# Attention's last steps, early compression weights, 32-row prompt norms and an earlier output projection in a hybrid decoder layer

## The chip, the cores and the metric

The kernel runs on one core of a Trainium2 chip, as one launch. The metric is the device time of the launch in microseconds; the table below has three runs and one profiled execution.

## The reference, cut to what matters

One inference step of one decoder layer, for a prompt of 512 tokens and for 8 samples of 4 tokens with 2048 past tokens. Every output is wanted in fp32.

```python
h = rmsnorm(x, w['g_mix'])
q, kc_new, ..., xm, vm, om, i_pre, f_pre = split_cols(h @ w['w_in'])
k_cmp = compress(kc_all, *w['cmp_k'])     # per 16-token block: two halves @ w1, gelu, @ w2
v_cmp = compress(vc_all, *w['cmp_v'])
o_nsa = nsa_attend(q, k_cmp, v_cmp, ks_all, vs_all, kw_all, vw_all, gates, offset, w_pre)
o_nsa = rmsnorm(o_nsa, w['g_head_nsa'])   # norm over the 64 columns of each of 8 heads
hm, C, n, m = mlstm_chunked(qm, km, vm, i_pre + w['b_i'], f_pre + w['b_f'], C0, n0, m0)
x = x + concatenate([o_nsa, gated_headnorm(hm)]) @ w['w_out']
x = x + cross_attention(rmsnorm(x, w['g_xa'])) @ w['w_xo']
x = x + swiglu(rmsnorm(x, w['g_ffn']))
```

`nsa_attend` adds three softmax attentions with gates: over compressed blocks, over selected 64-token blocks, over a window of 512. `mlstm_chunked` is a gated linear recurrence with 4 heads of 128.

## The kernel before, in words

**Numbers.** Products that must be exact to fp32 are made of three reduced-precision matmuls. `split(hi, lo, src)` (L212) writes a rounded copy `hi` on ACT (L213) and the rest `lo` on DVE or POOL (L214); `mm3` (L216) issues hi·hi, lo·hi and hi·lo (L218 to L220). A weight tile of 128x1024 is thus split by one ACT and one DVE instruction before TensorE (PE) may use it.

**Order of the work.** A scheduler writes one list of instructions per engine, and every engine then runs its list strictly in order. Program order counts, `tc.high_priority(offset)` pulls a block ahead of it, and `tc.issue_after(ins)` holds a block behind an instruction. The stages are generators: `weave(bg, fg)` (L315) runs a background generator of dense matmuls and takes a step of a foreground generator whenever the credit allows it, so that vector work of one stage lies beside matmuls of another.

**Stages, by time in the profile.** Projections and prompt attention (0 to 240 us), the hand-over to the prompt's mLSTM and to `compress(0)` (230 to 258), the compression of the samples' keys and then values (`compress(0)`, `compress(1)`, 254 to 535) woven with the mLSTM of prompt and samples and with the samples' attention, the end of the samples' attention (535 to 591), the projection by `w_out`, cross-attention (about 700 to 835) and SwiGLU.

**Prompt attention, `nsa` (L603).** 32 units (j, i, br), that is four head pairs j, four query tiles i and two branches; each has two heads v. `score` makes scores on PE, their minimum on DVE (L621), the exponential on ACT (L623), and the scaling by gate and sum on POOL (L625, tile `sb`). `turned` transposes `sb` on PE (L634) and copies it to `PT` on ACT (L636). `value` multiplies `PT` with the values (L646). In each step of the loop the transposes of v = 1 come first, then the `value` of an earlier pair of units, then the transposes of v = 0. After a pair's fourth tile its result goes to `oF` (L208 by DVE in the profile).

**mLSTM, `mlstm` (L766).** `load_qk(h)` (L778) loads two 128x128 weights `wqk` of a head in one buffer; `proj` projects with them (L799, L802) and asks for the next head's when the second of the two is used. `gate` (L811, L817, L818) makes the decay matrix, L825 and L827 the scores.

**Compression, `compress(kv)` (L1121).** 8 blocks b (the samples) of 4 steps t. `weights(t)` (L1125) splits the 128x1024 weight of a step into `w1h` and `w1l` and adds its halves on POOL (`ws`, L1134). `produce(b, t)` (L1171) transposes the gathered block on DVE (`xf`, L1191), splits it into `xh` and `xl`, and adds halves on POOL (`xs`, L1198); the steps are produced two ahead of the matmuls (L218 to L220 and L1296). `prompt_cols` (L1166) reads the prompt's rows back from a scratch array in memory (`xf<-cd`, issued by SP) and transposes them (`ys`, L1168). In the last block of `compress(0)` SP also loads the values' weights (`wr`, L588).

**The samples' selected blocks, `sample` (L1418).** For each key/value head g: keys are transposed by PE (L1518) and copied to `kt` by ACT or DVE (`keys`, L206 or L208), multiplied with the queries (L1528), and 2048 columns go through four exponentials on ACT (L1701). Then, for each g, the probabilities are transposed (L1518) and copied to `PTs`, and multiplied with the gathered values (L1722).

**The prompt's norms, `finals_p` (L1391).** For each head pair j: the compressed branch by two matmuls of 64 rows (L1398), added to `oF` (L1401), squared on ACT (L1402) into 512 columns of a tile of 128x2048; a matmul with `bones` (L1407, ones on the two 64x64 diagonal blocks, scaled) makes the mean square, copied back by ACT (L1408). Then one logarithm (L1411) and one exponential (L1412) over 2048 columns, each with a load of its table, and four products on DVE (L1415). It runs between the values of g = 0 and of g = 1.

**Output projection.** `early_mix` (L1824) splits `oF` into the projection's moving operand (`mh`, `ml`), and the first half of the columns (hf = 0) is multiplied with the splits of `w_out` (`whi`, `wlo`); `close_sample` and `load_xT` (L1811) transpose the residual `x`.

## Time and profile before

| | us |
|---|---|
| three runs | 1231.31, 1234.45, 1232.87 (median 1232.87) |
| the profiled execution, its own time | 1243.24 |
| its span on the core | 1241.5 |
| PE busy (share of the span) | 1174.3 (95%) |
| VectorE (DVE), ScalarE (ACT), GpSimd (POOL) busy | 841.2, 612.4, 558.6 |
| mean granted clock of PE | 0.974 |

The profiled execution is 10.4 us above the median of the runs, and 1.7 us of its time lie outside the span. PE is busy nearly throughout, so one reads the places where it isn't: a window that shows its busy time below the window's length, or a granted clock (column PEclk) below 1.00. PEld is the load of the stationary operand and runs beside PE. "Waits" names what released an engine that had stood. In windows and groups "x8" counts instructions; a matmul of fp32 operands stands there as two.

### The profile page before, as it was taken

Reading aid. Unit: us, or ns where it says so; the run is one execution under the profiler, and the core shown is the slowest. Engines: PE = TensorE matmul, PEld = TensorE weight load, DVE = VectorE, ACT = ScalarE, POOL = GpSimd, SP = SyncE. Lnnn points to the kernel's source line nnn. Section 1 sums busy time; section 2 is a strip of 40 time slices with the busy share of each in tenths; the row PEclk is TensorE's granted clock in tenths of the full one; section 3 lists DMA queues with packets and bytes.
Section 4 is the critical chain, followed back from the end, with each engine's and each line's share of the span. In section 5 each row is a group of like instructions: output and inputs, shape, how many; then the busy total and the mean of one; then the engine's idle time right before and its main releaser. Section 6 shows DMA issues by size and latency. Waiting matters only on the chain.

```text
span 1241.5 us, 24581 instructions
## 1 busy us (share of the span) xinstructions
PE 1174.3 (95%) x9220; PEld 1066.7 (86%) x9220; DVE 841.2 (68%) x1901; ACT 612.4 (49%) x1414; POOL 558.6 (45%) x686
## 2 busy tenths in 40 slices
PE   7999999899997989988999989999899999999996
PEld 5998999588885878854999987599899999999996
DVE  6337683567787687653754756554998888888874
ACT  5235665745545444466542423342665565555452
POOL 1013353566666266542342100043885576476342
PEclk9999999899997999999999998999999999999998
DMA  7324240141253185566767298630032333322411
GB/s 232 102 53 105 86 153 1 51 137 44 78 171 115 42 283 176 178 227 205 206 135 171 83 239 288 231 128 2 1 119 86 103 96 107 106 94 77 137 52 73
DMA packets 141769, 154.30 MB, mean 124 GB/s; under 512 B 17449, under 2 KB 123689, under 8 KB 141394
## 3 DMA queue, kind: packets, MB, share of 16 engines
q1 hardware_dynamic: 131922, 119.17, 32.0%
q0 software_dynamic: 9728, 33.56, 8.3%
q8 instruction: 73, 1.20, 0.4%
q14 instruction: 46, 0.38, 0.1%
HBM read 141.67 MB, written 13.12 MB: 125 GB/s over the span
## 4 chain that ended last, share of the span: by engine, by line
PE 49%; DVE 8%; ACT 3%; DMA 2%; issue 2%; SPq 1%; POOL 1%; POOLq 0%; DVEq 0%; ACTq 0%
PE xc L2291 7%; PE xa L2291 7%; PE bd L2291 5%; PE tp L2291 5%; PE bd L220 3%; PE bd L219 3%; PE bd L218 3%; DVE sp L2231 1%; DMA mkv<-in_cache_mem_k 1%; PE xa L1296 1%; PE tp L1518 1%; PE bd L2190 1%; PE xa L218 1%; PE xa L219 1%; PE xa L220 1%
## 5 line engine op out<-in xcount | busy, mean ns | idle before, releaser
L214 POOL TENSOR_TENSOR al<-fraw,ah 128x512 fp32r<-128x512 f32 (+1 forms) x104 | 127.5, 1227 | 152.4 <-ACT ah L213 124.0
L213 ACT ACTIVATE whi<-wraw 128x1024 fp32r<-128x1024 f32 (+3 forms) x74 | 62.5, 890 | 57.5 <-DMA wraw<-in_w_xv 28.2
L214 DVE TENSOR_TENSOR wlo<-wraw,whi 128x1024 fp32r<-128x1024 f32 (+3 forms) x74 | 73.6, 1026 | 19.1 <-ACT whi L213 19.0
L213 ACT ACTIVATE ah<-fraw 128x512 fp32r<-128x512 f32 (+1 forms) x112 | 65.8, 593 | 38.0 <-PE xc L2291 11.8
L218 PE MATMUL bd<-w1h,xh 128*128 128x256 f32 x256 | 82.6, 325 | 0.9 <-issue 0.9
L220 PE MATMUL bd<-w1h,xl 128*128 128x256 f32 x256 | 75.6, 298 | 3.0 <-DVE xl L214 3.0
L1198 POOL TENSOR_TENSOR xs<-xf 128x256 f32<-128x256 f32 x64 | 55.8, 878 | 50.2 <-PE xa L1296 30.5
L219 PE MATMUL bd<-w1l,xh 128*128 128x256 f32 x256 | 75.7, 297 | 0.0
L1296 PE MATMUL xa<-ws,xs 128*128 128x256 f32 x256 | 71.2, 400 | 2.4 <-DVE bq L1470 1.3
L625 POOL TENSOR_SCALAR sb<-sb,rs,gat 128x128 f32<-128x128 f32 (+3 forms) x64 | 46.1, 724 | 54.4 <-DVE rs L624 40.2
L213 ACT ACTIVATE xh<-xf 128x512 fp32r<-128x512 f32 x64 | 40.0, 629 | 45.5 <-DVE xf L1191 20.0
L213 ACT ACTIVATE ah<-sp 128x512 fp32r<-128x512 f32 (+1 forms) x64 | 35.5, 555 | 50.1 <-DVE sp L2231 22.8
L220 PEld LDWEIGHTS bd<-w1h,xl 128*128 128x128 f32 x256 | 48.9, 192 | 6.4 <-DVE xl L214 3.8
L1296 PEld LDWEIGHTS xa<-ws,xs 128*128 128x128 f32 x256 | 46.5, 201 | 8.5 <-issue 2.9
L218 PEld LDWEIGHTS bd<-w1h,xh 128*128 128x128 f32 x256 | 49.1, 193 | 5.0 <-issue 3.9
L214 DVE TENSOR_TENSOR xl<-xf,xh 128x512 fp32r<-128x512 f32 x64 | 47.5, 746 | 8.6 <-ACT xh L213 7.7
L219 PEld LDWEIGHTS bd<-w1l,xh 128*128 128x128 f32 x256 | 49.4, 193 | 4.5 <-issue 2.8
L219 PE MATMUL bd<-hlo,whi 128*128 128x272 f32 x176 | 52.0, 296 | 0.0
L218 PE MATMUL bd<-hhi,whi 128*128 128x272 f32 x176 | 51.7, 294 | 0.0
L1191 DVE STREAM_TRANSPOSE xf<-cgat 128x512 f32<-128x512 f32 x64 | 44.7, 703 | 10.2 <-POOL xs L1198 8.4
L220 PE MATMUL bd<-hhi,wlo 128*128 128x272 f32 x176 | 51.3, 292 | 0.0
L2231 DVE TENSOR_TENSOR sp<-fraw 128x512 f32<-128x512 f32 (+1 forms) x32 | 47.8, 1494 | 0.2
(990 smaller groups left out, 4667.9 us busy)
## 6 DMA issues: line engine op xcount, KB each, us to landing
fraw<-in_w_gate SPq DMA_DIRECT2D x11, 1024.0 KB
fraw<-in_w_up SPq DMA_DIRECT2D x11, 1024.0 KB
fraw<-in_w_down SPq DMA_DIRECT2D x24, 384.0 KB
mkv<-in_cache_mem_k SPq DMA_DIRECT2D x64, 128.0 KB
mkv<-in_cache_mem_v SPq DMA_DIRECT2D x16, 512.0 KB
wraw<-in_w_in SPq DMA_DIRECT2D x8, 512.0 KB
wraw<-in_w_xq SPq DMA_DIRECT2D x4, 1024.0 KB
wraw<-in_w_xk SPq DMA_DIRECT2D x4, 1024.0 KB
```

What stands on the lines that cost most here:

```text
L213: nc.scalar.activation(hi, src, AF.Copy)
L214: (eng or nc.gpsimd).tensor_tensor(lo, src, hi, op=OP.subtract)
L218: nc.tensor.matmul(out, ah, bh, start=first, stop=False, **kw)
L219: nc.tensor.matmul(out, ah, bl, start=False, stop=False, **kw)
L220: nc.tensor.matmul(out, al, bh, start=False, stop=last, **kw)
L625: (nc.vector, nc.gpsimd)[1].tensor_scalar(sb[:, :n], sb[:, :n], rs, gat[:, i, 3 * h + 1 + br:3 * h + 2 + br], op0=OP.mult, op1=OP.mult)
L1191: nc.vector.transpose(xf.rearrange("p a (q i) -> p q a i", q=4), gs[0].rearrange("p (q t a i) -> p t q a i", q=4, t=4, a=4)[:, t])
L1198: nc.gpsimd.tensor_tensor(xs_.rearrange("p c (v j) -> p v c j", v=2), xg[:, 0], xg[:, 1], op=OP.add)
L1296: nc.tensor.matmul(dst[2], ops[2][:, kk], w1s[t][2][:, kk], start=t == 0 and kk == 0, stop=t == 3 and kk == 1, skip_group_check=True)
L1518: nc.tensor.transpose(p[:, 128 * i:128 * i + 128], srcs(i), ident)
L2231: nc.vector.tensor_tensor(o, a, b, op=op)
L2291: nc.tensor.matmul(p[:, :HALF], w[a][:, k], x[b_][:, k], start=first and k == 0 and i == 0, stop=last and k == n - 1 and i == 2, skip_grou ...
```

## The change

**1. Prompt attention.** In the last unit the v = 0 transposes come ahead of the `value` of the pair before. The copy of the last pair's result to `oF` is put off into `compress(0)`.

**2. Early compression weights.** In `compress(0)` the weights of steps 0 and 1 and the first two `produce` are put at high priority behind the last exponential of the attention (`nsx`); the weights of steps 2 and 3 follow the first split of data (`x0`). The tiles for them are reserved ahead, in a fixed order.

**3. mLSTM weights.** `wqk` gets two buffers; heads 0 and 1 are loaded at the start, and head h + 2 when head h is done.

**4. Norms in 32 rows per pair.** `finals_p` takes every fourth column of `bones` as a stationary operand of 32 columns, so that the mean squares of pair j fall into rows 32j to 32j + 31 of one tile `vt` of 128x512; they are copied by DVE. Logarithm and exponential then run over 512 columns. A matrix `spread` (built by four small matmuls and an ACT copy) brings each pair's 32 rows back to 128 by one more matmul of 512 columns per pair, and the product reads that from PSUM. The steps are taken in the key loop of g = 0, and what is left of them after it, no longer between the two value groups.

**5. Projection among the values.** `early_mix` is written ahead of the rest of the foreground, held behind the second marked key copy of g = 1 (`cgs["kt"][1]`), and the splits of the first two chunks of `w_out` behind the third. The residual's tiles 3 to 5 are loaded and transposed later, in `close_sample`.

```diff
 def value(j, i):
...
-                if i == 3:
+                if j == 3 and i == 3:
+                    cgs["ev"] = acc.pop(j)
+                elif i == 3:
                     evac(oF[:, j, :512], acc.pop(j))
...
                     with tc.high_priority(offset=300), tc.issue_after(turned(*units[n - 1], 1)):
+                        if n == len(units):
+                            turned(*units[n - 1], 0)
                         if n > 2 and n % 2 == 0:
                             value(*units[n - 4][:2])
-                        turned(*units[n - 1], 0)
+                        if n < len(units):
+                            turned(*units[n - 1], 0)
...
-                wqk[h] = mq.tile([128, 2, 128], F32, name="wqk")
+                wqk[h] = mq.tile([128, 2, 128], F32, name="wqk", bufs=2)
...
             load_qk(0)
+            load_qk(1)
...
-                if w and h < 3:
-                    load_qk(h + 1)
+                if w and h < 2:
+                    load_qk(h + 2)
...
-            weights(0, raws[0])
+            if kv == 0:
+                with tc.high_priority(offset=2000), tc.issue_after(cgs["nsx"].ins):
+                    for t in range(2):
+                        weights(t, raws[t])
+            else:
+                weights(0, raws[0])
...
-                if b == 0 and t > 0:
+                if b == 0 and t > 0 and kv:
                     weights(t, raws[t])
+                elif b == 0 and t > 1:
+                    with tc.issue_after(cgs["x0"].ins):
+                        weights(t, raws[t])
...
+            if kv == 0:
+                with tc.high_priority(offset=2000), tc.issue_after(cgs["nsx"].ins):
+                    for i in range(2):
+                        produce(*steps[i])
+                evac(oF[:, 3, :512], cgs.pop("ev"))
...
+        def finals_p(sq, vt, spread):
             yield from need(("p", 1))
+            p = bank(ppo)
             for j in range(4):
+                nc.tensor.matmul(p[32 * j:32 * j + 32, :128], bones[:, 0:128:4], ident, start=True, stop=True)
+            nc.scalar.activation(spread, p[:, :128], AF.Copy, scale=4.0)
+            yield
+            for j in range(4):
+                js = slice(32 * j, 32 * j + 32)
+                acc = bank(ppo)
+                for v in range(2):
+                    nc.tensor.matmul(acc[64 * v:64 * v + 64], vcP[js, v], PcT[js, v], start=True, stop=True)
+                oj = oF[:, j, :512]
+                nc.vector.tensor_tensor(oj, oj, acc, op=OP.add)
+                nc.scalar.activation(sq, oj, AF.Square)
+                yield
+                p = bank(ppo)
+                nc.tensor.matmul(p[js], bones[:, 0:128:4], sq, start=True, stop=True)
+                nc.vector.tensor_copy(vt[js], p[js])
+                yield
+            nc.scalar.activation(vt, vt, AF.Ln, bias=eps_t)
+            nc.scalar.activation(vt, vt, AF.Exp, scale=-0.5)
+            yield
+            for j in range(4):
+                js = slice(32 * j, 32 * j + 32)
+                p = bank(ppo)
+                nc.tensor.matmul(p, spread[js], vt[js], start=True, stop=True)
+                oj = oF[:, j, :512]
+                nc.vector.scalar_tensor_tensor(oj, oj, gh[:, j:j + 1], p, op0=OP.mult, op1=OP.mult)
+                yield
...
                         if q % 2:
                             yield
+                            yield next(fp, None)
+                            next(fp, None)
...
-                if g == 0:
-                    yield from finals_p(sc.tile([128, 2080], F32, name="SS", bufs=2))
...
         def early_mix():
-            hot["wp"] = push("wp", bufs=2, side="right")
             hot[0] = [wt.tile([128, KT, HALF], R32, name=f"m{c}", bufs=1) for c in "hl"]
-            for k in (4, 5, 6, 7, 0, 1, 2, 3):
-                split(hot[0][0][:, k], hot[0][1][:, k], oF[:, k, :HALF], nc.gpsimd if k % 2 else nc.vector)
+            with tc.issue_after(cgs["kt"][1].ins):
+                for k in (4, 5, 6, 7, 0, 1, 2, 3):
+                    split(hot[0][0][:, k], hot[0][1][:, k], oF[:, k, :HALF], nc.gpsimd if k % 2 else nc.vector)
             fetch_x((2, 3), cgat_x())
-            fetch_x((4, 5), cgat_x())
-            for i in range(5):
+            for i in range(3):
                 load_xT(i)
...
+        early_mix()
         drain(fg)
         flip[1] = 2
-        early_mix()
...
+        def split_o(w):
+            with tc.issue_after(cgs["kt"][2].ins):
+                return split_w(w)
```

The added lines move the later ones of the file: L634 becomes L635, L646 becomes L647, L799 becomes L816, L802 becomes L819, L811 becomes L828, L218 to L220 become L219 to L221, L1518 becomes L1555, L1528 becomes L1568, L1722 becomes L1768, L1701 becomes L1745.

**First place: PE at the end of the prompt attention.** `tp<-ident,sb` are transposes, `xc<-PT,kvn` values of the attention, `tp<-xc,wqk` mLSTM projections, `bd<-w1h,xh` the first matmuls of the compression. Before:

```order
L811 MATMUL po<-M_3220,nsel 128x512
L634 MATMUL tp<-ident,sb 128x128 x4
L646 MATMUL xc<-PT,kvn 64x128 x12
L634 MATMUL tp<-ident,sb 128x128 x4
L646 MATMUL xc<-PT,kvn 64x128 x8
L799 MATMUL tp<-xc,wqk 128x512
L646 MATMUL xc<-PT,kvn 64x128 x8
L802 MATMUL tp<-xc,wqk 128x32
L799 MATMUL tp<-xc,wqk 128x512
L811 MATMUL po<-M_3220,nsel 128x512
L802 MATMUL tp<-xc,wqk 128x32
L799 MATMUL tp<-xc,wqk 128x512
```

And in the change:

```order
L635 MATMUL tp<-ident,sb 128x128 x8
L647 MATMUL xc<-PT,kvn 64x128 x28
L816 MATMUL tp<-xc,wqk 128x512
L819 MATMUL tp<-xc,wqk 128x32
L828 MATMUL po<-M_3235,nsel 128x512
L816 MATMUL tp<-xc,wqk 128x512
L819 MATMUL tp<-xc,wqk 128x32
L219 MATMUL bd<-w1h_3360,xh 128x256
L220 MATMUL bd<-w1l_3361,xh 128x256
L221 MATMUL bd<-w1h_3360,xl 128x256
```

The last two sets of four transposes now stand together, all 28 values follow without a projection between them, and the first three compression matmuls stand behind the second L819, where before two more projections, a gate and scores came first.

**Second place: DVE there.** `w1l` are the low parts of the weights, `ys` the transposed rows of the prompt. Before:

```order
L208 COPY oF<-xc 128x512
L210 TENSOR_SCALAR ksT<-tp 128x32
L1150 TENSOR_SCALAR w_3348<-w_3348 128x128
L214 TENSOR_TENSOR w1l_3343<-cgat,w1h_3342 128x1024
L214 TENSOR_TENSOR w1l_3385<-cgat,w1h_3384 128x1024
L214 TENSOR_TENSOR w1l_3406<-vcn,w1h_3405 128x1024
L214 TENSOR_TENSOR w1l_3504<-po_3201,w1h_3503 128x512
L1191 STREAM_TRANSPOSE xf<-cgat 128x4x4x32
L1159 STREAM_TRANSPOSE peT<-hidt 128x288
L1168 STREAM_TRANSPOSE ys<-xf 128x512
```

And in the change:

```order
L214 TENSOR_TENSOR w1l_3361<-cgat,w1h_3360 128x1024
L1216 STREAM_TRANSPOSE xf<-cgat 128x4x4x32
L214 TENSOR_TENSOR w1l_3367<-cgat,w1h_3366 128x1024
L1172 TENSOR_SCALAR w_3372<-w_3372 128x128
L1190 STREAM_TRANSPOSE ys<-xf 128x512
L1216 STREAM_TRANSPOSE xf<-cgat 128x4x4x32
L214 TENSOR_TENSOR xl<-xf,xh 128x2x4x64
```

The copy to `oF` has left the head of this piece (it is on ACT now); two instead of four weight pieces stand ahead of the first `xl`, and `ys` does too.

**Third place: PE at the samples' last values.** `po<-gat,PTs` are values, `sp<-PcT,vcP` and `tp<-SS,bones` the prompt's norms, `xa<-mh,whi` the projection by `w_out`. Before:

```order
L1398 MATMUL sp<-PcT,vcP 64x512 x2
L1722 MATMUL po<-gat,PTs 32x128 x16
L1407 MATMUL tp<-SS,bones 128x512
L1722 MATMUL po<-gat,PTs 32x128 x16
L1735 MATMUL po<-kvs,PN 128x128
L1398 MATMUL sp<-PcT,vcP 64x512 x2
L1407 MATMUL tp<-SS,bones 128x512
L1398 MATMUL sp<-PcT,vcP 64x512 x2
L1407 MATMUL tp<-SS,bones 128x512
L1749 MATMUL sp<-vcn,po_3201 32x128 x4
L1407 MATMUL tp<-SS,bones 128x512
```

And in the change, first at the last keys, then at the first values:

```order
L1555 MATMUL tp<-ident,gat 128x128 x8
L1450 MATMUL po<-SW,GX 128x512
L1555 MATMUL tp<-ident,gat 128x128 x4
L1450 MATMUL po<-SW,GX 128x512
L1568 MATMUL sp<-kt,Qn 32x512 x4
L1555 MATMUL tp<-ident,gat 128x128 x4
L1273 MATMUL xc<-w_5325,hid 127x64 x4
L1555 MATMUL tp<-ident,gat 128x128 x4
L1450 MATMUL po<-SW,GX 128x512
L1555 MATMUL tp<-ident,gat 128x128 x4
```

```order
L1568 MATMUL sp<-kt,Qn 32x512 x4
L1555 MATMUL tp<-ident,SS 128x128 x4
L219 MATMUL xa<-mh,whi 128x272
L220 MATMUL xa<-ml,whi 128x272
L219 MATMUL bd<-mh,whi 128x272
L220 MATMUL bd<-ml,whi 128x272
L219 MATMUL xc<-mh,whi 128x272
```

The `spread` matmuls (L1450; a fourth follows three rows later) now stand among the last keys' transposes, no piece of the norms is left among the values, and 21 matmuls of the projection stand ahead of the first value; 73 of the 192 of hf = 0 stand ahead of the last.

## Rows read from the trace of the kernel before

**Rows 1.** Windows at the hand-over to compression; first line: the columns
```profile
core 0: us, PE busy (x) PEld busy (x) DVE busy (x) ACT busy (x) POOL busy (x), PEclk, DMA share, GB/s
230.00:234.00 4.00, 1.88 (x12) 1.33 (x13) 1.89 (x5) 2.23 (x6) 2.29 (x4) 1.00 0.29 82
234.00:238.00 4.00, 4.00 (x34) 3.18 (x34) 0.00 (x0) 0.60 (x1) 3.87 (x5) 0.57 0.00 1
238.00:242.00 4.00, 4.00 (x38) 2.44 (x38) 0.69 (x1) 2.49 (x6) 0.47 (x2) 1.00 0.00 0
242.00:246.00 4.00, 2.00 (x6) 0.99 (x5) 2.89 (x4) 4.00 (x8) 1.90 (x4) 0.79 0.12 34
246.00:250.00 4.00, 4.00 (x8) 2.06 (x7) 3.09 (x6) 3.67 (x10) 2.28 (x3) 0.50 0.38 122
250.00:254.00 4.00, 2.92 (x11) 1.31 (x10) 4.00 (x6) 1.42 (x3) 3.68 (x7) 0.86 0.72 202
```

**Rows 2.** PE's waits in 215–260 us: total, times, longest
```profile
PE tp L799 <- DMA wqk<-in_w_qm: 1.9, 1, 1.9
PE bd L220 <- DVE xl L214: 1.1, 1, 1.1
```

**Rows 3.** Timeline of DVE, POOL and SP there: start us, duration us, instruction
```profile
249.95 0.71 DVE L1168 STREAM_TRANSPOSE ys<-xf 128x512 f32<-128x512 f32 x1 [0.91 <-DMA xf<-cd]
...
232.90 0.77 POOL L625 TENSOR_SCALAR sb<-sb,rs,gat 128x512 f32<-128x512 f32 x1 [0.20 <-DVE rs L624]
...
235.78 0.52 SPq L1157 DMA_DIRECT2D hidt<-in_cmp_b_k  x1
243.10 0.33 SPq L781 DMA_DIRECT2D wqk<-in_w_qm  x1
...
245.07 0.54 SPq L1167 DMA_DIRECT2D xf<-cd  x1
```

**Rows 4.** Windows of the samples' last keys and values, columns as rows 1
```profile
541.00:549.00 8.00, 5.37 (x30) 3.09 (x28) 2.47 (x7) 6.22 (x16) 3.32 (x6) 0.79 0.87 342
549.00:561.00 12.00, 9.17 (x71) 5.13 (x68) 9.02 (x14) 8.61 (x16) 8.11 (x8) 1.00 0.69 221
561.00:569.00 8.00, 7.31 (x116) 4.16 (x115) 4.13 (x13) 5.83 (x15) 1.87 (x2) 1.00 1.04 294
569.00:589.00 20.00, 15.20 (x177) 8.03 (x177) 4.87 (x12) 12.64 (x19) 4.33 (x5) 1.00 0.47 173
```

**Rows 5.** PE's waits in 525–605 us
```profile
PE po L1722 <- ACT PTs L206: 3.7, 2, 3.1
PE sp L1528 <- ACT kt L206: 3.0, 2, 2.6
...
PE po L1722 <- issue: 1.1, 3, 0.4
```

**Rows 6.** Groups by line and form in 525–606 us: busy us, mean ns, idle before
```profile
L213 ACT ACTIVATE whi<-wraw 128x1024 fp32r<-128x1024 f32 x8 | 8.2, 1057 | 3.5 <-DMA wraw<-in_w_out 3.5
...
L213 ACT ACTIVATE mh<-oF 128x272 fp32r<-128x272 f32 x8 | 3.1, 425 | 0.7 <-DVE oF L1415 0.6
...
L1402 ACT ACTIVATE SS<-oF 128x512 f32<-128x512 f32 x4 | 2.5, 626 | 3.9 <-DVE oF L1401 3.9
...
L1411 ACT ACTIVATE SS<-SS,eps_t 128x2048 f32<-128x2048 f32 x1 | 2.0, 2001 | 0.0
...
L1411 ACT ACT_TABLE_LOAD x1 | 1.3, 1283 | 0.0
```

**Rows 7.** Chain of waits, 525–606 us: start, us, engine and line
```profile
576.59 1.06 PE tp L1407 x2
```

**Rows 8.** Windows of the hand-over from keys' to values' compression, columns as rows 1
```profile
380.00:390.00 10.00, 5.24 (x49) 3.98 (x48) 9.91 (x19) 6.44 (x14) 8.77 (x8) 0.71 0.34 103
390.00:410.00 20.00, 16.47 (x85) 13.12 (x81) 10.79 (x21) 11.70 (x28) 6.31 (x6) 0.63 0.23 76
```

**Rows 9.** Timeline of SP there
```profile
381.06 7.02 SPq L588 DMA_DIRECT2D wr<-in_cmp_w_v  x8
```

76 lines of the change are left out of this document (39 added, 37 removed).

## The prediction

> **What bounds the kernel now.** I read the page first: PE is busy 95% of the span, so the end is set by PE wherever it is full, and only a place where it stands, or runs at the lower of its two clock levels (1.2 instead of 2.4 GHz, 0.50 in the column), can be shortened without taking work away. Next I read PE's busy time and clock in windows along the span; then, for the windows with gaps, PE's waits and the timelines of the engines it waits for; last the groups by line and form, for the price of single instructions. I count as lost in a window what PE stood, plus its busy time times one minus the clock. Three places that the change touches have such losses.
>
> **The hand-over, 230 to 254 us** [rows 1]. The six windows lose 2.12 us (standing), 1.72 (4.00 at clock 0.57), nothing, 2.42, 2.00 (4.00 at 0.50) and 1.49: 9.75 together. In 246 to 250 only 8 matmuls ran. Two waits are named [rows 2]: 1.9 us for mLSTM weights that were still on their way, and 1.1 for the low part of the data.
>
> **The samples' last keys and values, 541 to 589** [rows 4]. Standing takes 2.63 us in the first window, with 1.13 more by the clock of 0.79, then 2.83, 0.69 and 4.80: 12.1 together. PE waits there for ACT above all: 3.7 us for copied probabilities, of them 3.1 at once, and 3.0 for copied keys [rows 5]. The norms' logarithm over 2048 columns (2.00 us, and 1.28 for its table [rows 6]) is one of the instructions that stand on ACT among those copies.
>
> **From keys' to values' compression, 380 to 410** [rows 8]. 5.24 busy of 10 us at clock 0.71 and 16.47 of 20 at 0.63 are 8.3 us of standing and 7.6 of clock. The change does not rewrite this place, but moves it.
>
> **Part A: the hand-over** (items 1 to 3 of the change). What is to be kept: the last weighted scores leave POOL at 232.90 + 0.77 = 233.67 [rows 3]. The new PE order waits for them before its last values, so the 2.12 and 1.72 us of the first two windows stay. The extra cost of doing the v = 0 transposes first is nothing: PE has no other work ready in that gap, and if it had, the price would be the four transposes, a small part of a microsecond.
>
> What goes: the 1.9 us for `wqk`. The loads of head 1 were held up on SP's list until 243.10, though SP had been done with the row ahead at 235.78 + 0.52 [rows 3]; with two buffers they are issued with those of head 0. Their two more DMAs stand ahead of the other small loads of the compression on SP, at 0.33 us for the one shown, in a stretch where SP then idles anyway.
>
> What is prepared earlier: ACT was busy 0.60 us of 234 to 238 and full in 242 to 246 with the weights' high parts; DVE was idle in the first and had 2.89 in the second [rows 1]. The change moves two weight pieces, the first data and their low parts into that idle stretch. What then comes last for the first triple of compression matmuls? On DVE `ys` stands ahead of the first `xl`, and it needs the prompt's rows. These were issued at 245.07 and released DVE at 249.95, 4.88 us later [rows 3]. With SP free of the wait, I estimate the issue at 235.5, the landing at 240.4, and after three DVE instructions of 0.7 us each `xl` at 242.5. PE's own work of this piece, values, projections and a gate, kept it full from 234 to 242 (4.00 and 4.00 [rows 1]), so it is through at about 242 again. So of the 5.91 us lost from 242 to 254 some 0.6 remain: **A = -5.3 us**. Its bounds: only the `wqk` wait goes (-1.9), or all but the first window's standing goes, half clock included (-7.6).
>
> **Part B: the keys-to-values hand-over.** The values' weights are issued at 381.06 for 7 us [rows 9], behind the rows of `compress(0)`'s last block on SP in both orders. If compression runs 5 us earlier they are issued 5 us earlier. But the mLSTM and the samples' state, with which it is woven, don't all move along. I take 0, with 3 us either way: about a fifth of the 15.9 lost there.
>
> **Part C: norms and projection** (items 4 and 5). Removed: from 569 to 589 no piece of the norms lies between values any more, and projection matmuls, whose operands are ready, stand there instead: -4.80. The same matmuls lie in 561 to 569 (-0.69), and half of the 2.83 of 549 to 561 should go with them (-1.4); the other half is the burst of splits (eight of 0.43 and four of 1.06 us [rows 6]) that now stands before the first of them. That is -6.9.
>
> Added on PE: four `spread` matmuls of 512 columns, at 1.06 each by the matmul with `bones` of the same columns [rows 7], are 4.2; the building matmuls are four of 128 columns, by a quarter of that 0.27 each, or 1.1 at most, and I take 0.6. The sums of squares keep their price: 512 columns stream through in any case, and that the result has 32 rows saves nothing. So 4.8 of work; but the `spread` matmuls stand among the last keys' transposes, where PE stood 2.63 us [rows 4], so I charge 2.2. Added on ACT ahead of key copies: logarithm and exponential at about 0.6 each (between 2.00/4 and the 0.63 of a square of this shape), each with a table load of 1.28 [rows 6]: 3.8 in all if PE waits for both, 0 if it has matmuls; I take half, 1.9. Four copies moved from ACT to DVE and four products that read PSUM lie beside PE work: DVE is busy 2.47 of 8 us there [rows 4]; without that cover each is about the 0.71 of `ys`, a DVE instruction of 512 columns [rows 3]. **C = -6.9 + 2.2 + 1.9 = -2.8 us.** Bounds: -7.3 (every loss in the four windows gone, 4.8 of work added) to +5.5 (only the 4.80 goes, all of the 4.8, the 3.8 and 1.7 for four more splits in the burst are paid).
>
> A rule of the Trainium skill speaks against this part. The row first: between values of 32 rows and other matmuls PE stood for no named reason three times, 1.1 us in all and 0.4 at most [rows 5]. The skill's TensorEngine Tiling (Array Packing), Tiling Modes, Key Properties, says that changing the tiling mode, not merely the tile, drains the engine. The new norms come in 13 groups of matmuls of other shapes than their neighbours, up to 26 changes where there were 8. At 0.4 each, 18 more changes would cost 7.2 us; by the row's total hardly 1. I go by the total, and leave it within the bounds.
>
> **Later stages**: the residual's transposes come later but remain as many; the loads ahead of cross-attention shift by a few places. I take 0.
>
> **Sum**: -5.3 - 2.8 = -8.1 us on the profiled execution's 1243.24, that is 1235.1, or 0.65%. That execution lies 10.4 us above the median of the runs; scaled to the median, 1232.87 x 1235.1 / 1243.24 = 1224.8. I predict **1225 us**.
>
> **The rivals.**
> 1. *The lead is lost again at the keys-to-values hand-over.* Compression gets there 5.3 us earlier, but waits there for what the mLSTM and the samples bring. For it: 15.9 us are lost there with DVE busy 9.91 of 10 us [rows 8]. Against: the weights' loads move along. It leaves C alone: 1230.
> 2. *The early steps don't become early.* `ys` holds `xl` back as before, if the prompt's rows are issued no earlier, or the last copy to `oF` and the gate keep ACT from the first data. Only the 1.9 us of `wqk` goes, and C: 1228. Here the change doesn't do what it says.
> 3. *Slower: ACT starves the keys and values.* Squares (4 x 0.63), logarithm, exponential and loads (3.8), eight splits of `oF` (3.4) and four of `w_out` (4.2) are 13.9 us [rows 6], now all ahead of copies that PE awaits, in strict order; the projection matmuls stand in PE's list ahead of the first value and themselves wait for that burst. If PE waits for all of it, C is +13.9 + 4.8 - 4.8 and with A the sum is +8.6: 1241. It decides from where PE's waits for key and probability copies exceed today's 6.7 us [rows 5] by about 10. Against it: ACT is busy 12.64 of the 20 us of 569 to 589, and its total work falls.
> 4. *Both gains in full*: A -7.6 and C -7.3, the half clock included: 1218.
> 5. *Draining at each change of shape*, 7.2 us on the forecast, as worked out above: 1232. The rule named there is the skill's; the trace's 0.4 at most, three times, hardly bears it out.
>
> **How the numbers follow.** About 0.3%, 3.7 us, is what a measurement of this kernel can tell from no change: faster is below 1229.2, slower above 1236.6. Forecast 0.38, rival 1 0.17, rival 2 0.14, rival 3 0.14, rival 4 0.12, rival 5 0.05. Faster takes nine tenths of the forecast, rival 4, six tenths of rival 2 and a third of rival 1: 0.60. Slower is rival 3 and little else: 0.15. The same is left 0.25. The range runs from 1216, just under rival 4, to 1239: it takes in rivals 1, 2 and 5, and B's 3 us around the forecast, and leaves out most of rival 3.
>
> **What would show it.** Right: no wait for `wqk`; the first compression matmul near 243, and no window at 0.50 before compression is full; no norm matmul among the values, projection matmuls in every gap of them, and PE's waits for probability copies below 1 us. The prediction is wrong if the lost time from 380 to 410 grows by what the hand-over gained, if PE waits over 15 us for key and probability copies, or if cross-attention takes 3 us more.

## The result, and the profile after

| | median, us | runs | ratio to before, 95% interval |
|---|---|---|---|
| before | 1234.45 | 7 (1231.31 to 1238.04) | |
| after | 1240.72 | 7 (1237.1 to 1248.39) | 1.0064 [1.0038, 1.009] |

The change makes the kernel slower by 0.64%, where 0.65% faster was forecast. 1240.72 us lies just above the range of 1216 to 1239. The profiled execution of after is at the median: 1240.72 us, span 1238.7, PE busy 1176.8 us at a mean clock of 0.973. Before's profiled execution was a long one (1243.24); a second one of the same kernel, in run b1 below, took 1236.65 and is the one compared with.

**The hand-over.** Windows of after, columns as [rows 1]; then PE's longest wait there, and the timelines of SP, POOL and DVE:

```profile
234.00:238.00 4.00, 4.00 (x39) 3.67 (x39) 0.96 (x1) 3.13 (x5) 2.05 (x2) 0.58 0.01 4
...
242.00:246.00 4.00, 0.99 (x6) 0.54 (x4) 1.76 (x3) 3.78 (x8) 3.52 (x8) 0.77 0.27 91
246.00:250.00 4.00, 2.89 (x12) 2.80 (x13) 4.00 (x6) 1.69 (x5) 3.36 (x4) 0.50 0.65 191
250.00:254.00 4.00, 4.00 (x18) 2.79 (x17) 4.00 (x8) 0.00 (x0) 3.32 (x6) 0.88 0.39 119
```

```profile
PE bd L221 <- DVE xl L214: 4.1, 1, 4.1
```

```profile
239.50 1.13 PE L816 MATMUL tp<-xc,wqk 128*128 128x512 f32 x2
242.51 0.36 PE L219 MATMUL bd<-w1h,xh 128*128 128x256 f32 x1
...
239.68 0.38 SPq L1171 DMA_DIRECT2D w<-in_cmp_w_k  x1
240.16 0.53 SPq L1189 DMA_DIRECT2D xf<-cd  x1
...
239.69 0.34 POOL L1174 MEMSET hidt<- 128x288 f32 x1 [3.64 <-PE xc L647]
...
245.03 0.71 DVE L1190 STREAM_TRANSPOSE ys<-xf 128x512 f32<-128x512 f32 x1 [2.20 <-DMA xf<-cd]
...
246.41 0.65 DVE L214 TENSOR_TENSOR xl<-xf,xh 128x512 fp32r<-128x512 f32 x1
```

The wait for `wqk` of [rows 2] is gone, and the first compression matmul starts at 242.51. But then PE stands 4.1 us for `xl` (1.1 in [rows 2]). The prompt's rows were issued at 240.16, not at the 235.5 of the estimate, and released `ys` 4.87 us later; `xl` stands behind `ys`. SP's two loads and POOL's memset all start at 239.68 to 240.16, as soon as the last values of the attention are through (PE goes on to L816 at 239.50, and the memset names L647 as what it waited for). So the new tiles had to wait for the end of the attention. That it is memory which the values still held is inferred.

**Keys to values.** b1's windows first, then after's, columns as [rows 8]:

```profile
380.00:390.00 10.00, 4.30 (x30) 3.01 (x30) 9.91 (x21) 6.66 (x14) 8.76 (x8) 0.68 0.43 134
390.00:410.00 20.00, 17.72 (x111) 14.41 (x110) 11.96 (x23) 10.74 (x26) 5.99 (x7) 0.73 0.15 53
...
440.00:460.00 20.00, 15.82 (x115) 13.80 (x114) 15.94 (x60) 7.00 (x16) 12.13 (x22) 0.83 0.96 339
```

```profile
380.00:390.00 10.00, 2.72 (x22) 1.77 (x22) 7.12 (x24) 1.54 (x4) 6.14 (x8) 0.53 0.50 144
390.00:410.00 20.00, 18.87 (x105) 14.49 (x106) 13.11 (x29) 13.84 (x34) 7.45 (x8) 0.64 0.16 52
...
440.00:460.00 20.00, 18.73 (x164) 16.86 (x163) 19.29 (x64) 9.42 (x18) 16.22 (x25) 1.00 0.95 336
```

More stands and more runs at the lower clock before 410 (16.5 us lost in after's two windows, 14.1 in b1's), and it comes back after 440.

**The samples' last keys and values.** After's windows as [rows 4], and PE's waits as [rows 5]:

```profile
541.00:549.00 8.00, 5.07 (x17) 2.40 (x15) 3.54 (x10) 7.00 (x16) 0.10 (x1) 0.72 0.75 252
549.00:561.00 12.00, 11.92 (x56) 5.83 (x56) 4.98 (x9) 4.20 (x9) 3.76 (x4) 0.76 0.48 148
561.00:569.00 8.00, 5.36 (x38) 3.38 (x39) 5.03 (x10) 5.81 (x15) 3.87 (x5) 0.96 0.47 153
569.00:589.00 20.00, 20.00 (x245) 16.95 (x247) 11.01 (x18) 12.42 (x24) 8.55 (x10) 0.93 0.76 261
```

```profile
PE tp L1555 <- ACT kt L206: 4.4, 2, 2.4
PE tp L1555 <- DVE kt L208: 1.0, 2, 0.8
```

The wait for `PTs` is gone and 569 to 589 is full, as forecast. In its place PE waits for keys, and the first two windows run at 0.72 and 0.76.

**Time lost by stage.** To compare stages, each matmul is priced at the gap to the next start that matmuls of its operands show when nothing disturbs them (the 30th percentile of those gaps, the lowest of the kernels shown). A window's length minus these prices is the time lost in it, by standing, clock or switching (us; kernels as below):

| window | b1 (before) | eA | after | c2 (after) | gV | gNV |
|---|---|---|---|---|---|---|
| 230 to 262 | 18.2 | 16.4 | 16.4 | 17.5 | 17.1 | 17.6 |
| 262 to 380 | 22.7 | 25.8 | 25.9 | 25.3 | 25.2 | 25.3 |
| 380 to 440 | 18.7 | 22.1 | 20.7 | 21.9 | 21.6 | 21.9 |
| 440 to 460 | 9.1 | 2.7 | 3.9 | 3.3 | 3.7 | 2.9 |
| 460 to 540 | 14.9 | 17.2 | 14.7 | 16.8 | 15.5 | 16.0 |
| 540 to 620 | 30.8 | 35.7 | 28.3 | 29.9 | 34.6 | 27.1 |
| 620 to 760 | 19.3 | 19.5 | 20.5 | 19.1 | 20.7 | 20.0 |
| 760 to 820 | 13.5 | 13.3 | 17.3 | 17.9 | 12.6 | 12.6 |
| priced work in all | 1016.1 | 1015.6 | 1019.4 | 1019.4 | 1019.4 | 1019.7 |

These are estimates, and good for differences only. The last window matters: cross-attention, which the change doesn't rewrite, loses 4 us more from 760 on. From 540 to 620 single executions of one program differ by several us: after and c2 lose 28.3 and 29.9 there, with 10.2 us in a row at half the clock, and c1, a third execution of it, spent 23.9 us in a row there at half the clock.

### The profile page after: what moved, and what is told of

Its sections match the earlier page's. It is cut to its first block, busy times and chain, and to the rows that moved or that the text cites. A ratio compares the mean times of both kernels' runs of the same rounds, so it can differ in the third digit from the quotient of the medians.

```text
span 1238.7 us, 24621 instructions
## 1 busy us (share of the span) xinstructions
PE 1176.8 (95%) x9236; PEld 1066.6 (86%) x9236; DVE 848.5 (69%) x1902; ACT 609.5 (49%) x1414; POOL 562.7 (45%) x686
## 4 chain that ended last, share of the span: by engine, by line
PE 49%; DVE 7%; DMA 3%; ACT 2%; issue 2%; SPq 1%; POOL 0%; POOLq 0%; DVEq 0%; ACTq 0%
PE xc L2343 7%; PE xa L2343 7%; PE bd L2343 5%; PE tp L2343 5%; PE bd L220 3%; PE bd L219 3%; PE bd L221 3%; PE tp L1555 2%; PE xa L1329 2%; DMA mkv<-in_cache_mem_k 1%; PE bd L2242 1%; DVE sp L2283 1%; PE po L2192 1%; PE sp L1568 1%; PE xa L219 1%
## 5 line engine op out<-in xcount | busy, mean ns | idle before, releaser
L219 PE MATMUL bd<-w1h,xh 128*128 128x256 f32 x256 | 82.1, 321 | 2.3 <-ACT cur L1337 2.3
L221 PE MATMUL bd<-w1h,xl 128*128 128x256 f32 x256 | 75.1, 296 | 5.0 <-DVE xl L214 5.0
L220 PE MATMUL bd<-w1l,xh 128*128 128x256 f32 x256 | 76.3, 299 | 0.0
L1329 PE MATMUL xa<-ws,xs 128*128 128x256 f32 x256 | 67.9, 390 | 0.0
L219 PEld LDWEIGHTS bd<-w1h,xh 128*128 128x128 f32 x256 | 49.5, 193 | 8.1 <-ACT cur L1337 3.1
L221 PEld LDWEIGHTS bd<-w1h,xl 128*128 128x128 f32 x256 | 49.2, 193 | 8.1 <-DVE xl L214 5.4
L220 PEld LDWEIGHTS bd<-w1l,xh 128*128 128x128 f32 x256 | 49.5, 193 | 3.2 <-issue 2.1
L220 PE MATMUL bd<-hlo,whi 128*128 128x272 f32 x176 | 52.1, 296 | 0.0
L219 PE MATMUL bd<-hhi,whi 128*128 128x272 f32 x176 | 51.8, 294 | 0.0
L221 PE MATMUL bd<-hhi,wlo 128*128 128x272 f32 x176 | 51.3, 292 | 0.0
L214 DVE TENSOR_TENSOR al<-sp,ah 128x512 fp32r<-128x512 f32 (+1 forms) x64 | 40.8, 637 | 10.0 <-ACT ah L213 8.6
```

The lines of the kernel that those rows point to most:

```text
L214: (eng or nc.gpsimd).tensor_tensor(lo, src, hi, op=OP.subtract)
L219: nc.tensor.matmul(out, ah, bh, start=first, stop=False, **kw)
L220: nc.tensor.matmul(out, ah, bl, start=False, stop=False, **kw)
L221: nc.tensor.matmul(out, al, bh, start=False, stop=last, **kw)
L1329: nc.tensor.matmul(dst[2], ops[2][:, kk], w1s[t][2][:, kk], start=t == 0 and kk == 0, stop=t == 3 and kk == 1, skip_group_check=True)
```

## The experiments

Each ratio is to the kernel before on the same chip in the same call.

| run | median, us | before there | ratio, 95% interval |
|---|---|---|---|
| b1 | 1237.71 | 1239.57 | 0.9986 [0.9966, 1.0006] |
| c1 | 1243.88 | 1239.57 | 1.0032 [1.0004, 1.006] |
| eA | 1241.99 | 1239.57 | 1.0012 [0.9986, 1.0037] |
| eAF | 1248.2 | 1239.57 | 1.008 [1.0054, 1.0107] |
| eX | 1244.13 | 1238.82 | 1.0046 [1.0024, 1.0067] |
| eN | 1237.87 | 1238.82 | 0.9994 [0.9976, 1.0013] |
| eO | 1262.8 | 1238.82 | 1.0172 [1.0139, 1.0204] |
| eFP | 1253.24 | 1238.82 | 1.0102 [1.0065, 1.0139] |
| eL | 1244.8 | 1234.76 | 1.0068 [1.0045, 1.0091] |
| eM | 1243.55 | 1234.76 | 1.0076 [1.005, 1.0102] |
| eLM | 1246.14 | 1234.76 | 1.0084 [1.0063, 1.0105] |
| bM | 1234.42 | 1234.76 | 0.9998 [0.9981, 1.0015] |
| c2 | 1244.84 | 1239.89 | 1.0047 [1.0022, 1.0071] |
| gV | 1239.92 | 1239.89 | 1.0002 [0.9979, 1.0025] |
| gNV | 1233.85 | 1239.89 | 0.9952 [0.9932, 0.9971] |
| bV | 1238.63 | 1239.89 | 0.9997 [0.9972, 1.0022] |
| gQV | 1224.43 | 1233.73 | 0.9933 [0.9912, 0.9953] |

### The parts of the change: b1, c1, eA, eAF, eFP

b1 is the kernel before, c1 the whole change; eA has items 1 to 3 alone, eAF items 1 to 4, and eFP items 4 and 5 without 1 to 3 (each by leaving the other pieces of the diff above out).

> The kernel before, once more, for a second profile of it. The first one was 1243 us where its runs lie from 1231 to 1238. Both theories expect a ratio of 1.000 within 0.3%, and a profile whose lost time differs from the first profile's in one or two places by some 5 to 10 us: the place from 360 to 460 us (key compression's end and the gathers behind it) and cross-attention are the likeliest, since transfers end waits there.

> The whole change, once more, beside its parts on one chip. The ratio should come out at 1.003 to 1.009. If the spread of its own runs (1237 to 1248) is a matter of the chip it ran on, it is narrower here.

> Items 1 to 3 alone (attention's last steps, early compression weights, two buffers for the mLSTM weights); norms and projection as before. Theory 1, the hand-over's lead is real and lasts: 0.994 to 0.997 (4 to 7 us less). Theory 2, the lead is lost where keys' compression ends, in 365 to 410 us: 0.999 to 1.002, with the first compression matmul some 7 us earlier and the first values' compression matmul not earlier at all. If it is slower than 1.003, the hand-over costs time by itself, and neither theory holds.

> Items 1 to 4: as eA, and the norms in 32 rows per pair woven into the key loop; the output projection as before. Theory 1, the cost lies in the norms' place among the keys (more matmuls, logarithm and exponential ahead of key copies): 5 us or more above eA. Theory 3, the cost lies in the projection among the values and in the later order of loads: level with eA or up to 4 us below it, as the norms no longer stand among the values.

> Items 4 and 5 without items 1 to 3: norms among the keys and projection among the values, the hand-over as before. If the parts add up (items 1 to 3 at 1.0012, all at 1.0032): about 1.002. If the compression's early lead is what puts the norms into a place without dense matmuls: below 0.999.

Items 1 to 3 alone give nothing: 1.0012. By the table 1.8 us fewer are lost up to 262, and this lead is still there at 460, where the sums from 230 on are 68.7 (b1) and 67.0 (eA): what is lost more up to 440 comes back by 460. It goes behind that, with 2.3 us more lost from 460 to 540 and 4.9 from 540 to 620, where executions differ by as much; what takes it there was not tried (from 569 to 589 eA's clock was 0.71, b1's 1.00). Item 4 costs 6 us (eA to eAF, 1241.99 to 1248.2), and the projection of item 5 gives 4 back (eAF to c1). The parts don't simply add: without items 1 to 3 the rest stands at 1.0102, with them at 1.0032 to 1.0064 in the other calls. Why items that gain nothing alone help the others by some 5 to 9 us is not settled.

### Is it `ys` ahead of `xl`? eX

On items 1 to 3 alone, the transposes of the prompt's rows and a scaling are put behind the first `xl`:

```diff
-                nc.vector.transpose(dst, pcn)
+                tardy.append(lambda: nc.vector.transpose(dst, pcn))
...
+                    with tc.issue_after(lo_.ins):
+                        for f in tardy:
+                            f()
```

> Items 1 to 3 as in eA, with the prompt's rows (ys), the scaling of w2 and the small peT transposed on DVE behind the first low part xl, no longer ahead of it. In the changed kernel PE waited 4.1 us for that xl, which stood behind ys and its transfer. Theory 1 (that wait is what kept the hand-over from getting shorter): the wait falls below 1.5 us, the time that PE loses from 230 to 262 us falls by 2.5 to 4 us against eA. If the lead lasts, the ratio is 3 us below eA's 1.0012, at about 0.9985; theory 2 (a lead of the compression is lost where keys' compression ends) expects eA's ratio again, within 0.2%, with the loss grown in 360 to 440 us.

PE's waits and a window of eX:

```profile
PE sp L842 <- DVE xf L1222: 2.6, 1, 2.6
...
PE bd L221 <- DVE xl L1228: 0.7, 1, 0.7
```

```profile
246.00:250.00 4.00, 3.96 (x13) 2.38 (x13) 4.00 (x7) 1.09 (x5) 3.09 (x4) 0.87 0.46 130
```

The wait for `xl` falls from 4.1 to 0.7 us, and a wait of 2.6 takes its place, again for DVE, which is full from 246 to 250. The time doesn't fall (1.0046). Taking the wait away moves it on. That DVE's own list is the limit of this piece is read from the full window; no run shortened that list.

### ACT among the keys: eN, eL, eO

eN leaves out the logarithm and the exponential (two lines) and nothing else. eL keeps them but holds them behind a key copy of g = 1, the one marked last when they are written, and takes the steps behind them in the key loop of g = 1. eO takes the kernel before with the new norms in the old place, between the values of the two groups.

```diff
-            nc.scalar.activation(vt, vt, AF.Ln, bias=eps_t)
-            nc.scalar.activation(vt, vt, AF.Exp, scale=-0.5)
+            with tc.issue_after(cgs["kt"][-1].ins):
+                nc.scalar.activation(vt, vt, AF.Ln, bias=eps_t)
+                nc.scalar.activation(vt, vt, AF.Exp, scale=-0.5)
```

> The whole change without the prompt norms' logarithm and exponential (two ACT instructions over 512 columns; the prompt's norm is left out with them). In the changed kernel they and their table loads stand ahead of key copies, PE waits 4.4 us there and then runs 10 to 24 us at half clock. Theory 1 (that wait and the half clock behind it are the cost of the norms' place): PE's longest wait for a key copy falls below 1.5 us, little or no half clock is left between 540 and 580, and the time falls by 5 to 9 us against the whole change, to about 0.997. Theory 3 (the cost lies in the added matmuls and in the later stages): within 2 us of the whole change's 1.0032.

> The whole change with the norms' logarithm and exponential held behind the first marked key copy of the second key/value head, so that they no longer share ACT with the four long exponentials of the first; the spread matmuls follow later. Leaving both instructions out had taken the ratio from 1.0032 to 0.9994. Theory 1 (their place ahead of a key copy, with the four exponentials, is the cost): most of that comes back, 0.998 to 1.001, and PE's longest wait for a key copy in 520 to 620 us falls below 2 us. Theory 1b (the two instructions and their table loads cost wherever they stand among the keys): 1.002 to 1.004.

> The kernel before with the norms in their new form (32 rows per pair, 512 columns), but in their old place between the two value groups. Theory 1 (the place costs, the form gains): 0.997 to 1.000, as logarithm and exponential are 2.7 us shorter there and four matmuls more cost up to 4.8. If the form by itself costs: 1.003 or more.

First ACT's and PE's timelines in the whole change (c1), with two of its windows (columns as [rows 1]); then the same windows without the two functions (eN):

```profile
540.54 1.28 ACT L1444 ACT_TABLE_LOAD   x1
541.84 0.72 ACT L1444 ACTIVATE SW<-SW,eps_t 128x512 f32<-128x512 f32 x1
...
543.11 1.28 ACT L1747 ACT_TABLE_LOAD   x1
...
544.72 0.58 ACT L206 ACTIVATE kt<-tp 128x512 f32<-128x512 f32 x1
...
545.35 0.94 PE L1555 MATMUL tp<-ident,gat 128*128 128x128 f32 x4 [2.06 <-ACT kt L206]
547.07 1.11 PE L1555 MATMUL tp<-ident,gat 128*128 128x128 f32 x4 [0.78 <-DVE kt L208]
548.12 2.07 PE L1450 MATMUL po<-SW,GX 32*128 32x512 f32 x2
...
549.00:561.00 12.00, 12.00 (x36) 5.55 (x35) 4.02 (x9) 2.59 (x6) 2.83 (x3) 0.50 0.34 107
561.00:569.00 8.00, 8.00 (x31) 4.25 (x29) 2.44 (x5) 3.38 (x7) 0.94 (x1) 0.50 0.40 124
```

```profile
549.00:561.00 12.00, 10.20 (x74) 6.31 (x73) 5.83 (x12) 7.78 (x19) 5.72 (x6) 1.00 0.67 222
561.00:569.00 8.00, 6.98 (x70) 4.46 (x74) 7.09 (x7) 6.63 (x11) 4.19 (x5) 0.79 0.54 188
```

In c1 the two functions and the two table loads take 3.9 us of ACT (1.28 + 0.72 + 1.28 + 0.62). The second load stands ahead of the samples' own exponentials (L1747), and the norm's exponential runs among these without one. A key copy waits behind the second load, and PE stands twice. From 549 to 569 the clock then is at 0.50, with 67 matmuls in 20 us that PE shows as wholly busy: two records of a `spread` matmul take 2.07 us, where the matmul of 512 columns in [rows 7] took 1.06. eN does 144 matmuls in the same time. So two waits of 2.8 us together are followed by 20 us at half the clock; c2, with the same program, was at 0.57 for 12 us. In all seven profiles with the functions at this place (after, c1, c2, eAF, eFP, eM, gV) a stretch of 10.2 or 23.9 us at half the clock starts between 543 and 551; in eN and gNV, which leave them out, and in before and b1 none from 530 to 600 is longer than 3.4. eA, with the old norms among the values, has one of 13.7 that starts later, at 567, so the functions are not the only thing that brings the clock down there. Without the functions the ratio is 0.9994, 0.004 below c1's and 0.005 below c2's: some 5 us.

PE's waits of eL (525 to 605 us), then a window and the longest waits of eO (560 to 620):

```profile
PE po L1451 <- DVE oF L1453: 2.4, 1, 2.4
PE tp L1556 <- ACT kt L206: 1.9, 2, 1.3
PE po L1451 <- ACT SW L1446: 1.3, 1, 1.3
```

```profile
580.00:600.00 20.00, 10.92 (x16) 1.66 (x16) 4.65 (x8) 7.10 (x11) 1.48 (x2) 0.50 0.14 35
...
PE po L1408 <- ACT r L1405: 5.8, 4, 1.5
...
PE po L1417 <- ACT SW L1412: 3.5, 1, 3.5
```

eL halves the wait for keys, but its `spread` matmuls wait 3.7 us instead: no gain (1.0068). eO, at 1.0172, is some 21 us slower, with 16 matmuls in 20 us: between the values nothing stands between the steps of the new form, whose one square and one bank make each pair wait for the one before. So the new form needs other work between its steps; that there is too little of it among the keys is argued, not shown.

### Cross-attention: eM, eLM, bM, then gV, bV, gNV, c2

Two candidates were left for the loss after 620: the loads, since SP's list now has the third piece of `w_xv` behind 62 instead of 58 memory-key loads; and the samples' value products (`po<-mkv` in their second run), which the scheduler now cuts into 15 groups between matmuls of other shapes, where before had 9. One product is 128 rows by 32 columns, and four in a row write four different strips of 32 rows of the result. eM holds the memory loads behind the `w_xv` loads that they should follow, eLM is eL and eM together, bM does it to the kernel before.

```diff
-                        nc.sync.dma_start(t_[32 * h:32 * h + 32].rearrange("p (q d) -> p q d", q=8), src[h])
+                        if held_w[0] is not None:
+                            with tc.issue_after(held_w[0].ins):
+                                nc.sync.dma_start(t_[32 * h:32 * h + 32].rearrange("p (q d) -> p q d", q=8), src[h])
```

> The whole change with the loads of the samples' memory keys held behind the loads of w_xv that come ahead of them in the program. In all kernels with the new norms the third piece of w_xv stands behind 62 of these loads on SP, in the others behind 58, and PE loses some 34.5 us from 700 to 820 us where it lost 30 without. Theory 4 (a shifted order of loads in cross-attention costs 4 to 5 us of the change): PE's waits for w_xv (6 us in the changed kernel) fall below 3, the loss in this stretch falls by 3 to 6 us and the ratio to about 0.999. If the loss there comes from elsewhere (the order of small matmuls): the ratio stays above 1.002.

> Both of the above in one kernel. If the two costs are separate: their gains add, about 0.995. If one of the theories falls: the better one's ratio alone.

> The kernel before with the memory loads held in the same way. Here the third piece of w_xv stood behind 58 loads. Theory 4 says that the place of these loads matters by itself: 0.997 to 0.999. If before's order is as good as any: 0.999 to 1.002.

The loads move, in eM PE's waits for the splits of the weights from 700 on shrink to 2.4 us (b1 3.5, after 6.6), and a wait of 3.1 us for the memory's tiles comes instead; nothing is gained (1.0076, 1.0084, 0.9998), and the 15 groups stay.

gV regroups: the 16 products of one pair of loads stand in a block at high priority, which leaves 6 groups. bV does this to the kernel before, gNV to eN.

```diff
+                    with tc.high_priority(offset=200):
                         for a in range(2):
                             for bp in range(4):
...
                     if h % 2:
                         for _ in range(4):
                             mem_load()
-                    yield
+                        yield
+                        yield
```

> The whole change once more, as the reference for the other three on this chip. Every theory says the same: a ratio of 1.003 to 1.0065 to the kernel before, some 4 to 8 us, with about 5 us more lost in cross-attention (620 to 820 us) than before and 15 groups of the samples' value products (po<-mkv in their second run) between matmuls of other shapes.

> The whole change, with the samples' 64 value products of cross-attention written as one block of 16 per pair of loads at high priority, so that PE takes them in 6 groups (4, 29, 1, 15, 1, 14) and no longer in 15; the loads of the memory keys and of w_xv keep their places. Theory 4b (the loss in cross-attention comes from the cut groups, each change between products of 32 rows and matmuls of 128 costing 0.3 to 0.5 us): 18 changes fewer, 3 to 5 us less between 760 and 820 us, and a ratio 0.003 to 0.004 below that of the whole change in this call. Theory 4a (it comes from the shifted loads that PE waits for): the groups go but the loss stays, and the ratio is that of the whole change within 0.001.

> The same regrouped cross-attention, and without the logarithm and the exponential of the prompt's norms (so the prompt's norm is left out of the result). If the two losses, ACT among the keys and the cut groups, are separate and both as measured or supposed so far (4.7 and 3 to 5 us), the ratio is 0.995 to 0.997, faster than the kernel before: then nothing else of weight is left. If the cut groups cost nothing it stays at 0.999 to 1.0 as without the two functions alone.

> The kernel before with the same regrouping: 9 groups become 6. Theory 4b: 6 changes fewer, 1 to 3 us, a ratio of 0.9975 to 0.999. If the high priority itself were what helps (the value products done earlier, whatever their grouping), the gain here is as large as for the whole change, 3 to 5 us, 0.996 to 0.9975. Theory 4a: 1.0.

The windows 770 to 820 of these matmuls alone (PE busy, PEld busy, clock, DMA share, GB/s), of b1, c2 and gV; then single groups in PE's timeline of c2, where two records are one product:

```profile
770.00:820.00 50.00, 9.99 (x128) 3.89 (x128) 1.00 0.59 198
```

```profile
770.00:820.00 50.00, 13.66 (x128) 4.64 (x128) 1.00 0.64 213
```

```profile
770.00:820.00 50.00, 9.37 (x128) 4.21 (x128) 1.00 0.67 231
```

```profile
779.95 0.64 PE L2192 MATMUL po<-mkv,Qx 128*32 128x256 f32 x8
...
781.80 1.93 PE L2192 MATMUL po<-mkv,Qx 128*32 128x256 f32 x30
...
789.41 0.63 PE L2192 MATMUL po<-mkv,Qx 128*32 128x256 f32 x6
...
791.95 0.62 PE L2192 MATMUL po<-mkv,Qx 128*32 128x256 f32 x2
792.50 0.33 PE L2235 MATMUL tp<-ident,pr 128*128 128x128 f32 x1
...
793.57 1.48 PE L2192 MATMUL po<-mkv,Qx 128*32 128x256 f32 x18
...
796.96 1.05 PE L2192 MATMUL po<-mkv,Qx 128*32 128x256 f32 x10
```

The same 128 records at full clock take 9.99 us in 9 groups, 13.66 in 15 and 9.37 in 6. The loads stayed as they were (PE's waits for these splits are 6.1 us in gV and 5.7 in c2), and gV is 4.9 us faster than c2 (4.3 of them in these records): the loss is the cut groups. bV, with 9 groups to start from, gains 1.3 us, within its interval. gNV is at 0.9952: with both causes away, the change is 6 us faster than before, though with two functions fewer than before.

The rows also say why a cut costs. One product takes 0.62 us, three 0.63 and four 0.64; five take 1.05, nine 1.48 and fifteen 1.93. So the time goes up by 0.43 us with every fourth product, and up to four products cost what one does. I read this as those for the four strips running beside each other; no run was made for it. A group of one, five or nine wastes three quarters of its last step. The 64 products make 19 such steps in b1 (groups of 4, 14, 3, 12, 3, 3, 10, 2 and 13) and in gV, and 25 in c2 (4, 15, 3, 1, 1, 1, 9, 1, 5, 1, 5, 1, 1, 1, 15). Between b1 and gV the steps are the same and three groups fewer save 0.62 us, 0.2 each; this is what is left of a group's time beside its steps. Six steps and six groups more in c2 are then 6 x 0.43 + 6 x 0.2 = 3.8 us, where 3.67 was measured. About two thirds of the loss are steps that weren't filled.

The Trainium skill's TensorEngine Tiling (Array Packing), Tiling Modes, Key Properties, says that changing the mode, not just the tile, drains the engine. Only the 0.2 us per group could be such a drain, and no run here tells it from the way the profile models a matmul's end.

### A version that beats both: gQV

gNV leaves out the norm. gQV keeps it, without a function of ACT. The squares become the stationary operand and two columns of `bones` the moving one, so that the mean squares stand in 32 columns of 128 rows. POOL raises them to -0.5, and after a DVE copy PE turns them back against the unit matrix. The regrouping of gV is in it.

```diff
-                nc.tensor.matmul(p[js], bones[:, 0:128:4], sq, start=True, stop=True)
-                nc.vector.tensor_copy(vt[js], p[js])
+                for i in range(4):
+                    nc.tensor.matmul(p[:, 2 * i:2 * i + 2], sq[:, 128 * i:128 * i + 128], bones[:, 0:128:64],
+                                     start=True, stop=True)
+                r8 = rr[:, 8 * j:8 * j + 8]
+                nc.vector.tensor_scalar(r8, p[:, :8], EPS, None, op0=OP.add)
+                nc.gpsimd.tensor_tensor(r8, r8, mhalf[:, :8], op=OP.pow)
...
-            nc.scalar.activation(vt, vt, AF.Ln, bias=eps_t)
-            nc.scalar.activation(vt, vt, AF.Exp, scale=-0.5)
...
-                nc.tensor.matmul(p, spread[js], vt[js], start=True, stop=True)
+                nc.vector.tensor_copy(vt.rearrange("p (n d) -> p n d", n=8),
+                                      rr[:, 8 * j:8 * j + 8, None].to_broadcast([128, 8, 64]))
+                for i in range(4):
+                    nc.tensor.matmul(p[:, 128 * i:128 * i + 128], vt[:, 128 * i:128 * i + 128], ident, start=True, stop=True)
```

> The whole change with the regrouped cross-attention, and with the prompt's norms kept, but without a logarithm, an exponential or a table on ACT: the squares are the stationary operand and two columns of bones the moving one, so that the 4096 mean squares fall into 32 columns of 128 rows; POOL raises them to -0.5 in four instructions of 8 columns (about 1.7 us each, estimated from 1.05 for 4 columns and 0.55 for one in the trace); DVE spreads them to 512 columns per pair, and PE turns them back by four matmuls of 128 columns. Theory (the two losses are ACT among the keys and the cut groups): within 0.002 of the run without the two functions, a ratio of 0.995 to 0.997, faster than both kernels. Rival (what cost the time is that norm work, of whatever engine, stands among the keys): PE waits for POOL's powers or DVE's copies there instead, a half clock of 10 us or more between 540 and 570, and 0.999 to 1.001.

Windows of gQV, then POOL's power and PE's longest wait in 535 to 620:

```profile
541.00:549.00 8.00, 7.65 (x70) 6.34 (x72) 4.53 (x10) 3.93 (x8) 2.88 (x3) 1.00 0.75 232
549.00:561.00 12.00, 9.59 (x87) 5.48 (x91) 9.69 (x13) 9.89 (x21) 7.43 (x9) 1.00 0.80 295
561.00:569.00 8.00, 8.00 (x93) 6.36 (x84) 5.68 (x11) 4.60 (x13) 1.41 (x1) 1.00 0.74 223
569.00:589.00 20.00, 20.00 (x301) 17.50 (x301) 5.78 (x13) 8.28 (x17) 7.14 (x8) 1.00 0.82 260
```

```profile
530.33 1.68 POOL L1442 TENSOR_TENSOR GX<-GX,mhalf 128x8 f32<-128x8 f32 x1
...
PE tp L1554 <- ACT kt L206: 1.9, 3, 1.4
```

All four windows are at full clock and the last is full. At 1224.43 us, 0.9933 [0.9912, 0.9953], it is faster than before (whose median was 1233.73 there) and than the change. The rival, that norm work among the keys costs whatever engine does it, falls. gQV also has no matmul with a 32-row operand left in the norms but those of the compressed branch, so how much of its gain is ACT and how much are changes of shape isn't told apart here.

## Why the prediction was wrong

**What held.** PE's end of the attention kept its stand, the wait for `wqk` went, the first compression matmul came at 242.51 ("near 243"), no norm matmul was left among the values, and the window of 569 to 589 filled up. Of the -6.9 put on norms leaving the values and the projection coming in, the projection alone gave 4.3 (eAF to c1). **Part B, put at 0**, held as well: 262 to 440 loses 6.5 us more in eA than in b1 (25.8 + 22.1 against 22.7 + 18.7), and 440 to 460 gives 6.4 back. gNV is at -6 us and gQV at -9.3, beside the forecast of -8.1, but gNV does two functions less than before and both have the regrouped products, so they don't bear out the forecast's way. Three terms failed.

**Part A, put at -5.3, gave nothing in the end.** The step that failed is "with SP free of the wait, I estimate the issue at 235.5": SP's place in the list was free, but the tiles were not before 239.7, so the rows came 4.7 us later than estimated and `ys` held `xl`, which is the wait that rival 2 named. The lead was 1.8 us by 262, about the 1.9 that rival 2 left of it. DVE, full from 246 to 250 even in eX, would probably have bounded it there anyway; the text priced DVE's three instructions for the first triple and not the list behind them. The lead of 1.8 us lasted to 460 and was lost after it, so rival 1 had the loss of a lead right, but not the place.

**Part C, the term "added on ACT", put at 1.9, is about 5 to 6.** eN against c1 is 0.0038, gNV against gV 0.005. The mechanism was named (ACT ahead of key copies) and its bound was the 3.8 us of the functions and loads. What was left out is that PE's stand there is followed by a stretch at half clock, 10.2 us long in after and 23.9 in c1, and the price exceeds all the time that ACT takes. Rival 3 had the right place and sign, and its 1241 us meets the measured time by luck: PE's waits for copies fell from 6.7 to 5.4 us, and it was to decide at 10 more. The work added on PE was 3.3 us by the priced sums, of 4.8 in the text's whole and 2.2 charged.

**"Later stages: I take 0"** cost 3.7 us against b1 in the value products of cross-attention (13.66 against 9.99). The change doesn't touch cross-attention, but the order there came out otherwise, with 15 groups where there were 9; that the scheduler's reckoning of all that stands ahead does this is inferred. Rival 5 had a cost of changes of shape, but neither its place nor its mechanism: a group beside its steps costs 0.2 us, not 0.4, and most of the loss is in groups that don't fill a step of four. Going by the row's total of 1.1 us, waits of no named reason, missed it, because the trace shows this time as PE busy. The order of the whole program would have shown the 15 groups before any run.

By the ratios, ACT's functions are 6.2 us (gV against gNV, 0.005 of 1239.89) and the groups 5.6 (c2 against gV, 0.0045; 4.9 by the medians). With gNV's -6 they make c2's +5.8; they must, as each is the step from one of these runs to the next, so the sum gives sizes and doesn't prove that nothing else is in it.

Two of the signs that the prediction named as proof against it came true: from 380 to 410 after loses 2.3 us more than b1, where the hand-over had gained 1.8, and cross-attention takes over 3 us more. **Open**: why items 1 to 3 help the rest, as said above, where their own lead goes after 460, and what memory the early tiles waited for.

## What to carry to other kernels

After a reordering, compare the order of all stages, also of those that the change doesn't name, and look at small products that share PE by strips: a group that is cut so that it doesn't fill a step of four costs busy time, and shows no wait. A short wait of PE can cost more than its length: in c1 2.8 us of waits were followed by 23.9 us at half the clock, so what stands on ACT ahead of copies that PE awaits is priced with the windows behind it. And an early place in a queue is worth nothing before the tile that the instruction writes is free.

## What the runs showed of the hardware

- Products of 128 rows by 32 columns, for four strips of a result in turn, took 0.62 us for one, 0.64 for four, 1.05 for five and 1.93 for fifteen (c2): four took the time of one, and a step of four 0.43. Cut into 15 groups and not 9, the same products took 3.67 us more, all shown as PE busy at full clock.
- The clock stayed at 0.50 for 20 us (c1, 549 to 569) while PE is shown as wholly busy, with 67 matmul records in that time.
- The logarithm took a table load of 1.28 us, and the next exponential another, with the next instruction right behind each (c1). The Trainium skill's ScalarE: Activation LUTs, Table sets: the hidden batching unit, names one set that holds both, so that one load would do; this kernel's program loads two, and no run tried the other.
- POOL's power took 1.68 us for 8 columns, where after's trace has 1.05 for 4 and 0.55 for one: about 0.16 us per column.
